# Routing stage of a PEER decoder layer: counts of five heads behind the last query, query 15 in token halves, both look-ups in one run, and the fill of W on ScalarE

## The chip, the cores and the metric

The kernel runs on one core of one Trainium2 chip. A core has a matrix engine (TensorE, here PE, with its weight loads PEld), a vector engine (VectorE, DVE), an activation engine (ScalarE, ACT), a general engine (GpSimd, POOL) and an engine that issues transfers (SyncE, SP). Each works through its own instructions in order and waits on semaphores for the others. The metric is the device time of one execution in microseconds (us), the median of several runs.

## The reference

One decoder layer on 256 tokens of width 2048. Attention (eight differential and eight stick-breaking heads), a product-key expert layer (PEER), and a gated embedding, each with a layer norm behind it. The change lies in the PEER layer, cut to this:

```python
q = (xt @ wq).reshape(t, PEER_HEADS, PEER_QDIM)            # 8 heads, 256 wide
sa = einsum('thc,nc->thn', q[..., :128], sub_keys[0])      # 128 scores for each half
sb = einsum('thc,nc->thn', q[..., 128:], sub_keys[1])
va, ia = top_k(sa, 16)
vb, ib = top_k(sb, 16)
cand = va[..., :, None] + vb[..., None, :]                 # 16 x 16 pairs
cidx = ia[..., :, None] * 128 + ib[..., None, :]
top, sel = top_k(cand, 16)
eidx = take_along_axis(cidx, sel)                          # 16 experts of 16384 per head
gates = softmax(top)
act = gelu(einsum('thed,td->the', u[eidx], x))
out = einsum('the,thed->td', gates * act, v[eidx])
```

## The kernel before, in words

Routing comes first: for each of 16 half-queries `hh` (8 heads, two keys each) `query(hh)` multiplies the 256 tokens with a block of `peer_wq` (16 matmuls of 256 columns, which the profile counts as 32 passes), ACT copies the result to `qT`, and `scores` multiplies it with the keys into `S`. On DVE `best_scores(hh)` finds the 16 best of 128 for two token tiles; with both keys of a head done, `best_pairs` finds the 16 best pairs and turns their places into the two indices of each expert. For that it makes a run of three operations for each key: compare the place with 0 to 15 (`equal`, tile `eqsel`), multiply with the indices found before (`TIh`), add up (`tensor_reduce`), into `iaN` or `ibN`. `head_slots` sends the indices of the first 32 tokens to `eig`.

Then the kernel counts which experts are wanted by which group of 32 tokens. POOL scales the indices (`apart`); PE spreads them (`sets_of`, tile `ps_iS`, the index matmuls); ACT copies them out as `a` and `nb`. DVE turns `a` into one-hot rows `oa` (`hots_out`, one `equal` of 3584 elements), ACT makes 28 rows `sb` of steps with Sign activations (`steps_up`), and `counted` adds their 28 products in `ps_cnt`, for all heads in the same three banks.

What sets the order: most of these instructions are kept in the order in which the program is written. The work behind a query is written as generators that the class `Background` runs at ticks. A tick follows each of the 16 matmuls of a query; `bg.add(work, delay)` makes the work due so many ticks later, and a generator that yields `n` goes on `n` ticks later. `hot_work(h)` is added behind query 2h+2 with a delay of 22+2h: the index matmuls at its start, then Sign rows at a tick each, then the counts, four per tick. After query 15 `bg.flush()` runs what is left. Head 6 is done by hand behind it, and head 7 by `last_hot`, where the compare of `a` and of the last step rows lies on DVE in pieces.

On DVE hots_out(h) stands behind best_scores(2h+3) and ahead of best_pairs(h+1).

Next comes the sorting of experts into blocks. `classes` copies the counts out (`below`), makes flags `f` where an expert is wanted, and combines them by token groups (`wh`, `nn`, `nm`, `I`). `offsets` and `running` add them up on PE (`ps_off`, `ps_run`), `lists` makes the indices `idx` of the experts of a block, and POOL gathers their rows by indirect DMA (`uf`). From there PE transposes each block (`ps_T`, copied by ACT to `uT`) and multiplies it with the tokens, block by block; the gelu goes into `W`, a tile of 42 x 224 elements per partition, which must hold ones before since the gates are multiplied in wherever they come. After that the same is done with the rows of `v`, and the layer ends.

The lines that matter: `query` from L810, `scores` L821, `best_pairs` L845, `hot_tiles` L981, `steps_up` L985, `hot_work` L998, `last_hot` L1018, `classes` L1046, the end of the loop (`bg.flush`) L1464 and the fill of `W` L1491. `W` is filled by one instruction on POOL:

```python
    nc.gpsimd.memset(W, 1.0)
    sorting = classes(flp, cnt, I, some)
    next(sorting)
```

`W` lies where tiles of the routing lay (pools `tk`, `tkl`), so it waits for the last of them, the transfer of head 7's `eg` to `eig`. Pools `lp` (with `I`, `run`, `io`) and `flp` are open beside `hotp` (with `sb`, `apart`), so that their tiles can be filled early. `oa` takes turns in three buffers `gb` that later hold gathered rows.

Of the kernel before, what the change touches and what calls it, by code (L numbers as in the profile page):

```python
# [20 lines left out]
P = 128  # L21
T = 256
# [30 lines left out]
ACT_LAST = 10  # L53
NCB = NKEY + 1
# [242 lines left out]
def build(tc, a, out):  # L297
# [512 lines left out]
    def query(hh):  # L810
        ps = pbank(pq, "ps_q", "q", 3)
        wf = su.load(a["peer_wq"][hh])
        for dt in range(ND):
            keep(nc.tensor.matmul(ps[:, :T], wf[:, dt * P:(dt + 1) * P], XF[:, dt],  # L814
                                  start=dt == 0, stop=dt == ND - 1))
            bg.tick()
        qT = tk.tile([P, T], F32, name="qT", tag="qT", bufs=2)
        keep(nc.scalar.copy(qT, ps[:, :T]))
        bg.add(scores(hh, qT), 2)

    def scores(hh, qT):  # L821
        pk = pbank(pq, "ps_k", "k", 1)
        for t in range(NT):
            keep(nc.tensor.matmul(pk[:, t * NKEY:(t + 1) * NKEY], qT[:, t * P:(t + 1) * P],
                                  keysT[:, hh % 2, :], start=True, stop=True))
        keep(nc.scalar.copy(S[:, hh // 2, :, hh % 2, :],
                            pk[:, :T].rearrange("p (t n) -> p t n", t=NT)))
        yield from ()
# [16 lines left out]
    def best_pairs(h0, n, then=None):  # L845

        q0, nq = NT * h0, NT * n
# [12 lines left out]
        for q in range(q0, q0 + nq):  # L860
            top16(tkl, CV[:, q], CI[:, q], cand[:, q - q0, :])
        ci = CI[:, qs].rearrange("p q k -> p (q k)")
        s4, s2 = (tkl.tile([P, 96], U32, name=nm)[:, :nk] for nm in ("by16", "by4"))
        pF, u1 = (tkl.tile([P, 96], F32, name=nm)[:, :nk] for nm in ("pF", "u1"))
        at = [tkl.tile([P, 96, 2], F16, name=f"at{which}")[:, :nk] for which in range(2)]
        two = [P, nk, 2]
# [10 lines left out]
        keep(nc.vector.scalar_tensor_tensor(
            at[1], pF[:, :, None].to_broadcast(two), -36.0, u1[:, :, None].to_broadcast(two),
            op0=ALU.add, op1=ALU.max))
        for which, dst in ((0, iaN), (1, ibN)):  # L880
            eq = tkl.tile([P, 96, TOPK], F16, name="eqsel", tag="eqsel", bufs=1)[:, :nk]
            equal(eq, io128[:, :TOPK], at[which])
            e4 = eq.rearrange("p (q k) i -> p q k i", k=TOPK)
            keep(nc.vector.tensor_tensor(
                e4, e4, TIh[:, qs, which, None, :].to_broadcast([P, nq, TOPK, TOPK]),
                op=ALU.mult))
            for h in range(n):
                keep(nc.vector.tensor_reduce(
                    dst[:, :, (h0 + h) * TOPK:(h0 + h + 1) * TOPK],
                    eq.rearrange("p (h t k) i -> p h t k i", t=NT, k=TOPK)[:, h],  # L890
                    axis=AX.X, op=ALU.add))
            if then:
                then(which)
        for h in range(h0, h0 + n):
            head_slots(h)
# [100 lines left out]
    hots = {}  # L996

    def hot_work(h, xa, xb):  # L998
# [3 lines left out]
        oa, sb = hot_tiles()  # L1002
        hots[h] = oa[:, :SETS], a2
# [14 lines left out]
    def last_hot(h):  # L1018

        oa, sb = hot_tiles()  # L1020
# [20 lines left out]
        best_pairs(h, 1, then)  # L1041
# [4 lines left out]
    def classes(flp, cnt, I, some):  # L1046

        f = flp.tile([P, 8, P], F16, name="f8")
        keep(nc.vector.memset(f[:, 0], 0.0))
        for ps, g, n in zip(cnt, (0, 3, 6), (3, 3, 1)):  # L1050
            v = ps[:, :n * NCB].rearrange("p (n b) -> p n b", n=n)
            keep(nc.scalar.copy(below[:, g:g + n], v))
            tt(f[:, 1 + g:1 + g + n], v[:, :, 1:], below[:, g:g + n, :P], ALU.is_gt)
        w = f
# [374 lines left out]
    for hh in range(2 * PH):  # L1429
        if hh == HEARLY:  # L1430
# [7 lines left out]
            iaN, ibN = (lsp.tile([P, NT, PH * TOPK], F32, name=nm) for nm in ("iaN", "ibN"))  # L1438
# [3 lines left out]
            lp = pools.open("lp", "right", bufs=1)  # L1442
            flp = pools.open("flp", "right", bufs=1)
# [9 lines left out]
        query(hh)  # L1453
        if hh:
            best_scores(hh - 1)
        if hh and hh % 2 == 0:
# [3 lines left out]
            best_pairs(h, 1)  # L1460
            xs = [apart(h, which, nc.gpsimd) for which in range(2)]
# [29 lines left out]
    nc.gpsimd.memset(W, 1.0)  # L1491
# [5 lines left out]
    for i, (k0, n) in enumerate(spread(K4, KR)):  # L1497
        running(k0, n, "TU"[i], i == 0)
# [814 lines left out]
```

## Time and profile before

| | |
|---|---|
| median of 3 runs | 1500.56 us (1498.18 to 1502.86) |
| the profiled execution | 1506.18 us |
| its span, first to last instruction | 1504.3 us |
| mean granted clock of TensorE | 0.97 |
| PE busy | 1404.7 us (93%) |
| DVE busy | 884.6 us (59%) |
| ACT busy | 656.6 us (44%) |
| POOL busy | 442.7 us (29%) |

Every time below is from one profiled execution, counted from its first instruction. PE is busy nearly all the time, and the two places in the page's row of 40 slices where it is not show where to look: slices 14 and 15, from about 530 to 600 us, with 7 and 4 tenths. The first routing query starts at 416.4 us, the last one's scores end at about 548.7, and the first block of expert rows is gathered at 588.18. In a row of the timeline stand start, duration, engine, line, operation, output and inputs, shapes, the count, and in brackets how long the engine had been idle and what ended that; a row can hold several instructions. In the chain of waits a row is a link: start, duration, what.

### The profile page before, as it was taken

Reading aid. Unit: us, or ns where it says so; the run is one execution under the profiler, and the core shown is the slowest. Engines: PE = TensorE matmul, PEld = TensorE weight load, DVE = VectorE, ACT = ScalarE, POOL = GpSimd, SP = SyncE. Lnnn points to the kernel's source line nnn. Section 1 sums busy time; section 2 is a strip of 40 time slices with the busy share of each in tenths; the row PEclk is TensorE's granted clock in tenths of the full one; section 3 lists DMA queues with packets and bytes.
Section 4 is the critical chain, followed back from the end, with each engine's and each line's share of the span. In section 5 each row is a group of like instructions: output and inputs, shape, how many; then the busy total and the mean of one; then the engine's idle time right before and its main releaser. Section 6 shows DMA issues by size and latency. Waiting matters only on the chain.

```text
span 1504.3 us, 32578 instructions
## 1 busy us (share of the span) xinstructions
PE 1404.7 (93%) x13216; PEld 1109.3 (74%) x13216; DVE 884.6 (59%) x2455; ACT 656.6 (44%) x1447; POOL 442.7 (29%) x413
## 2 busy tenths in 40 slices
PE   9999999999999974998999998999998999995898
PEld 7888888887888863997888887888985444331686
DVE  5456568875558887678856766787532000005767
ACT  5587646875325562543544454444550000003632
POOL 0033213310041114332433443443553444321000
PEclk9999999999999985999999999999999999997899
DMA  8655665548543204878799888999999999999471
GB/s 304 203 167 156 195 212 154 153 149 319 177 162 112 85 1 155 312 286 311 288 376 335 322 305 321 347 368 360 400 396 386 418 417 419 413 382 353 171 264 56
DMA packets 74733, 402.82 MB, mean 268 GB/s; under 512 B 10980, under 2 KB 13060, under 8 KB 36580
## 3 DMA queue, kind: packets, MB, share of 16 engines
q0 software_dynamic: 39280, 272.11, 46.6%
q1 hardware_dynamic: 33568, 125.42, 24.6%
q10 hardware_dynamic: 1728, 3.15, 0.6%
q8 instruction: 105, 1.72, 0.4%
q14 instruction: 52, 0.43, 0.1%
HBM read 404.97 MB, written 4.45 MB: 272 GB/s over the span
## 4 chain that ended last, share of the span: by engine, by line
PE 66%; DMA 11%; issue 10%; DVE 6%; POOL 4%; ACT 1%; POOLq 0%; ACTq 0%; DVEq 0%
PE ps_T L1528 9%; PE ps_qk L336 8%; PE ps_u L1551 7%; PE ps_q L814 7%; PE ps_u L1536 6%; PE ps_qk L338 4%; DMA vf<-v_rows,idx 4%; DMA vg<-v_rows,idx 2%; PE ps_v L355 2%; DMA vx<-v_rows,idx 2%; PE ps_v L357 2%; PE ps_v L356 2%; PE ps_gate L355 2%; PE ps_gate L357 2%; PE ps_gate L356 2%
## 5 line engine op out<-in xcount | busy, mean ns | idle before, releaser
L1530 ACT COPY uT<-ps_T 128x512 f32<-128x512 f32 x404 | 220.9, 615 | 288.5 <-PE ps_T L1528 264.3
L239 DVE TENSOR_TENSOR wl<-wf,wh 128x1024 fp32r<-128x1024 f32 (+1 forms) x167 | 192.9, 1169 | 104.1 <-ACT wh L238 102.6
L1503 POOL DMA_INDIRECT uf<-u_rows,idx x101 | 134.3, 1330 | 281.6 <-PE ps_T L1528 217.4
L1528 PE MATMUL ps_T<-ident,uf 128*128 128x128 f32 x1616 | 211.0, 276 | 0.3 <-issue 0.2
L238 ACT CAST wh<-wf 128x1024 fp32r<-128x1024 f32 (+1 forms) x167 | 155.0, 945 | 115.7 <-PE ps_v L357 34.0
L336 PE MATMUL ps_qk<-X,wh 128*128 128x512 f32 x512 | 185.2, 401 | 0.0
L1528 PEld LDWEIGHTS ps_T<-ident,uf 128*128 128x128 f32 x1616 | 181.5, 146 | 4.1 <-issue 3.3
L338 PE MATMUL ps_qk<-X,wl 128*128 128x256 f32 x512 | 145.7, 285 | 0.0
L1551 PE MATMUL ps_u<-uT,XF 128*32 128x128 f32 x3904 | 134.8, 277 | 9.0 <-issue 7.2
L1536 PE MATMUL ps_u<-XF,uT 128*128 128x128 f32 (+2 forms) x832 | 134.9, 314 | 7.9 <-ACT acts L1600 4.3
L1835 DVE BATCH_NORM_STATS2 st<-ps_v 128x6 f32<-128x512 f32 x8 | 5.6, 700 | 214.0 <-PE ps_v L1871 162.2
L1536 PEld LDWEIGHTS ps_u<-XF,uT 128*128 128x128 f32 x832 | 121.3, 194 | 10.6 <-ACT acts L1600 5.2
L1551 PEld LDWEIGHTS ps_u<-uT,XF 128*32 128x32 f32 x3904 | 105.3, 110 | 29.9 <-issue 21.8
L1788 PE MATMUL ps_v<-vf,W 128*32 128x512 f32 x936 | 107.6, 612 | 16.1 <-DMA vf<-v_rows,idx 16.1
L814 PE MATMUL ps_q<-XF,wf 128*128 128x256 f32 x512 | 121.9, 384 | 0.0
L336 PEld LDWEIGHTS ps_qk<-X,wh 128*128 128x128 f32 x512 | 96.4, 188 | 22.0 <-issue 1.0
L1262 DVE SCALAR_TENSOR_TENSOR junk<-io,ibF,ps_find 128x128 f16<-128x128 f16 x224 | 64.4, 344 | 74.1 <-PE ps_find L1254 61.0
L814 PEld LDWEIGHTS ps_q<-XF,wf 128*128 128x128 f32 x512 | 93.0, 190 | 10.4
L1788 PEld LDWEIGHTS ps_v<-vf,W 128*32 128x32 f32 x936 | 40.2, 111 | 80.8 <-issue 59.8
L1392 DVE SCALAR_TENSOR_TENSOR y<-gb,ew,y 128x2048 f32<-128x2048 f32 x31 | 72.8, 2349 | 45.5 <-DMA gb<-v_rows,eig 45.5
L338 PEld LDWEIGHTS ps_qk<-X,wl 128*128 128x128 f32 x512 | 96.3, 188 | 2.5 <-issue 1.3
L1788 PE MATMUL ps_v<-vx,W 128*32 128x512 f32 x672 | 74.3, 592 | 0.0
(364 smaller groups left out, 2505.0 us busy)
## 6 DMA issues: line engine op xcount, KB each, us to landing
wf<-w_qk SPq DMA_DIRECT2D x64, 512.0 KB
wf<-w_out SPq DMA_DIRECT2D x32, 512.0 KB
wf<-peer_wq SPq DMA_DIRECT2D x16, 1024.0 KB
wf<-ple_gate SPq DMA_DIRECT2D x16, 1024.0 KB
wf<-w_v SPq DMA_DIRECT2D x16, 512.0 KB
wf<-w_sv SPq DMA_DIRECT2D x15, 512.0 KB
iarow<-s_iar SPq DMA_DIRECT2D x14, 512.0 KB
x<-x SPq DMA_DIRECT2D x2, 1024.0 KB
```

What stands on the lines that cost most here:

```text
L238: self.order(nc.scalar.copy(wh, src))
L239: self.order(nc.vector.tensor_tensor(wl, src, wh.bitcast(F32), op=ALU.subtract))
L336: nc.tensor.matmul(ps, wh[:, j * P:(j + 1) * P], xt[:, dt, :], start=dt == 0, stop=False)
L338: nc.tensor.matmul(ps[:, :T], wl[:, j * P:(j + 1) * P], xt[:, dt, :T], start=False, stop=dt == ND - 1)
L814: keep(nc.tensor.matmul(ps[:, :T], wf[:, dt * P:(dt + 1) * P], XF[:, dt], start=dt == 0, stop=dt == ND - 1))
L1392: keep(nc.vector.scalar_tensor_tensor(ys, g, ew[:, j:j + 1], ys, op0=ALU.mult, op1=ALU.add))
L1503: keep(nc.gpsimd.indirect_dma_start(out=dst, out_offset=None, in_=src, in_offset=bass.IndirectOffsetOnAxis(ap=idx[:, col:col + 1], axis=0) ...
L1528: keep(nc.tensor.transpose(ps[:, j * P:(j + 1) * P], rows[i][:, (4 * c + j) * P:(4 * c + j + 1) * P], ident))
L1530: keep(nc.scalar.copy(turned[i][:, c * 512:(c + 1) * 512], ps))
L1536: keep(nc.tensor.matmul(ps[:, :n], uT[:, d * P:(d + 1) * P], groups_of(d, *block.wide), start=d == 0, stop=d == ND - 1))
L1551: keep(nc.tensor.matmul(ps[32 * q:32 * q + 32, w * P:(w + 1) * P], XF[:, d, t0:t0 + 32], uT[:, d * P:(d + 1) * P], start=first and not w, ...
L1788: keep(nc.tensor.matmul(ps[32 * j:32 * j + 32], w, vf[:, j * 512:(j + 1) * 512], start=False, stop=last))
```

## The change

Four edits.

1. The counts of heads 2 to 6 are no longer made by `hot_work` but kept in a list and made in one run of 140 matmuls behind the last scores. For that `sb` has five buffers in place of two, and heads 5 and 6 have an `oa` of their own. Head 6 goes through `hot_work` like the others, and the delays are 20+h in place of 22+2h.
2. Query 15 is made in two halves of 128 tokens, each with its own copy and scores, a tick at every second matmul. hots_out(6) now stands ahead of best_scores(15).
3. In `best_pairs` one run of three operations, twice as wide, finds the indices for both keys, in a common tile `iab`. Head 7 keeps two runs, since its work goes on behind the first.
4. `W` is filled with ones by ACT, in four copies of 2352 elements: two behind the copies of the counts, two behind the first `running`. The flags are made in a function of their own, ahead of the closing of `hotp`; `lp` and `flp` are opened behind it, on the same place, so the small fillings of `I` and `run` on POOL and the load of `io` on SP now stand behind the counts.

The places in the program's order, without times. First PE around query 14, from behind the index matmuls of head 4; `ps_q` are the query, `ps_k` the scores, `ps_cnt` the counts (of head 4, with `oa`), `ps_iS` the index matmuls (with `apart`). Before:

```order
L814 MATMUL ps_q<-XF,wf 128x256 x4
L824 MATMUL ps_k<-keysT,qT 128x128 x2
L814 MATMUL ps_q<-XF,wf 128x256 x16
L824 MATMUL ps_k<-keysT,qT 128x128 x2
L814 MATMUL ps_q<-XF,wf 128x256 x5
L992 LDWEIGHTS oa
L992 MATMUL ps_cnt<-sb,oa 128x129
```

Now:

```order
L818 MATMUL ps_q<-XF,wf 128x256 x10
L829 MATMUL ps_k<-keysT,qT 128x128 x2
L818 MATMUL ps_q<-XF,wf 128x256 x16
L829 MATMUL ps_k<-keysT,qT 128x128 x2
L818 MATMUL ps_q<-XF,wf 128x256 x7
L982 LDWEIGHTS apart
L982 MATMUL ps_iS<-eighth,apart 128x16
```

The counts of head 4 are gone from query 14, and the index matmuls of head 5 stand behind its ninth matmul (two ahead of the scores, seven behind); before they stood behind the sixteenth.

Second, PE at the last query. Before, where the index matmuls of head 5 end and the counts of head 5 begin:

```order
L967 MATMUL ps_iS<-eighth,apart 128x16
L814 MATMUL ps_q<-XF,wf 128x256 x2
L824 MATMUL ps_k<-keysT,qT 128x128 x2
L814 MATMUL ps_q<-XF,wf 128x256 x14
L824 MATMUL ps_k<-keysT,qT 128x128 x2
L992 LDWEIGHTS oa
L992 MATMUL ps_cnt<-sb,oa 128x129
```

Now, from the index matmuls of head 5 to those of head 6:

```order
L982 MATMUL ps_iS<-eighth,apart 128x16
L818 MATMUL ps_q<-XF,wf 128x256 x7
L818 MATMUL ps_q<-XF,wf 128x128 x4
L829 MATMUL ps_k<-keysT,qT 128x128 x2
L818 MATMUL ps_q<-XF,wf 128x128 x16
L829 MATMUL ps_k<-keysT,qT 128x128
L818 MATMUL ps_q<-XF,wf 128x128 x12
L829 MATMUL ps_k<-keysT,qT 128x128
L982 LDWEIGHTS apart
L982 MATMUL ps_iS<-eighth,apart 128x16
```

Query 15 has become 32 narrow matmuls with two scores, and the index matmuls of head 6 follow at once; the 140 counts stand behind these and ahead of the index matmuls of head 7.

Third, ACT behind the last counts (`below` copies them out). Before:

```order
L986 ACTIVATE sb<-ioh,nb 128x129 x10
L1052 COPY below<-ps_cnt 128x387 x2
L1052 COPY below<-ps_cnt 128x129
L1116 CAST run<-ps_run 128x4x128
L1530 COPY uT<-ps_T 128x512 x4
```

Now:

```order
L1004 ACTIVATE sb<-ioh,nb 128x129 x10
L1072 COPY below<-ps_cnt 128x387 x2
L1072 COPY below<-ps_cnt 128x129
L1520 COPY W<-one 128x2352 x2
L1139 CAST run<-ps_run 128x4x128
L1520 COPY W<-one 128x2352 x2
L1562 COPY uT<-ps_T 128x512 x4
```

Two pieces of `W` stand ahead of `run` and two ahead of the first `uT`; on POOL the memset of `W` is gone from between `eig` and the first gather.

The diff, cut to its core:

```diff
+LATER = 2
+OWN_OA = (5, 6)
...
+    def query(hh, step=NT):
         wf = su.load(a["peer_wq"][hh])
-        for dt in range(ND):
-            keep(nc.tensor.matmul(ps[:, :T], wf[:, dt * P:(dt + 1) * P], XF[:, dt],
-                                  start=dt == 0, stop=dt == ND - 1))
-            bg.tick()
...
+        for t0 in range(0, NT, step):
+            c = slice(t0 * P, (t0 + step) * P)
+            ps = pbank(pq, "ps_q", "q", 3)[:, :step * P]
+            for dt in range(ND):
+                keep(nc.tensor.matmul(ps, wf[:, dt * P:(dt + 1) * P], XF[:, dt, c],
+                                      start=dt == 0, stop=dt == ND - 1))
+                if step == NT or dt % 2:
+                    bg.tick()
...
+            bg.add(scores(hh, qT, range(t0, t0 + step)), 2)
...
+        else:
+            equal(eqsel, io128[:, :TOPK], at.rearrange("p w q k two -> p q w k two")
+                  .rearrange("p q w k two -> p (q w) k two"))
+            e4 = eqsel.rearrange("p (qw k) i -> p qw k i", k=TOPK)
             keep(nc.vector.tensor_tensor(
...
+                e4, e4, TIh[:, qs].rearrange("p q w i -> p (q w) i")[:, :, None, :]
+                .to_broadcast([P, 2 * nq, TOPK, TOPK]), op=ALU.mult))
+            keep(nc.vector.tensor_reduce(iab.rearrange("p q w c -> p (q w) c")[:, :, hs], e4,
+                                         axis=AX.X, op=ALU.add))
+        head_slots(h)
...
+    def hot_tiles(h):
+        if h in OWN_OA:
+            oa = hotp.tile([P, SETS, P], F16, name="oa", tag="oa", bufs=len(OWN_OA))
+        else:
+            oa = gin.tile([P, 32, P], F16, name="oa", tag="gb", bufs=NGB)[:, :SETS]
+        return oa, hotp.tile([P, SETS, NCB + 1], F16, name="sb", tag="sb", bufs=PH - LATER - 1)
...
+        if h >= LATER:
+            later.append((h, oa, sb))
+            return
         yield 3
         for s in range(0, SETS, 4):
             counted(h, oa, sb, s, s + 4)
...
-        query(hh)
+        query(hh, NT if hh < 2 * PH - 1 else 1)
...
-            if h < PH - 2:
-                bg.add(hot_work(h, *xs), 22 + 2 * h)
+            best_pairs(h)
+            bg.add(hot_work(h, *(apart(h, which, nc.gpsimd) for which in range(2))), 20 + h)
     bg.flush()
+    hots_out(PH - 2)
     best_scores(2 * PH - 1)
-    last = hot_work(PH - 2, *xs)
-    next(last)
-    hots_out(PH - 2)
-    for _ in last:
-        pass
+    for h, oa, sb in later:
+        counted(h, oa, sb, 0, SETS)
     last_hot(PH - 1)
...
+    flags(f8)
+    pools.close("hotp", "pq")
     pools.close("tk", "tkl")
+    lp = pools.open("lp", "right", bufs=1)
+    flp = pools.open("flp", "right", bufs=1)
...
-    nc.gpsimd.memset(W, 1.0)
-    sorting = classes(flp, cnt, I, some)
+
+    def fill(x0, x1):
+        n = NC * NDT // 4
+        for x in range(x0, x1):
+            keep(nc.scalar.copy(W.rearrange("p c n -> p (c n)")[:, x * n:(x + 1) * n],
+                                one.to_broadcast([P, n])))
+
+    fill(0, 2)
+    sorting = classes(flp, f8, I, some)
     next(sorting)
-    pools.close("hotp", "pq")
...
     for i, (k0, n) in enumerate(spread(K4, KR)):
         running(k0, n, "TU"[i], i == 0)
+    fill(2, 4)
```

More of the change, by code (lines that the diff above doesn't have):

```diff
@@ L843, in best_scores, with best_pairs @@
             top16(tk, TV[:, q, hh % 2, :], TI[:, q, hh % 2, :], S[:, hh // 2, t, hh % 2, :])
-    def best_pairs(h0, n, then=None):
-        q0, nq = NT * h0, NT * n
+    def best_pairs(h, then=None):
+        q0, nq = NT * h, NT
         qs, nk = slice(q0, q0 + nq), nq * TOPK
@@ L861, in best_pairs, with pair @@
             top16(tkl, CV[:, q], CI[:, q], cand[:, q - q0, :])
[L862 to L866, printed above, removed]
+        ci = CI[:, qs]
+        s4, s2 = (tkl.tile([P, nq, TOPK], U32, name=nm) for nm in ("by16", "by4"))
+        pF, u1 = (tkl.tile([P, nq, TOPK], F32, name=nm) for nm in ("pF", "u1"))
+        at = tkl.tile([P, 2 * nk, 2], F16, name="at")
+        at = at.rearrange("p (w q k) two -> p w q k two" if then else
+                          "p (q w k) two -> p w q k two", w=2, k=TOPK)
+        two = [P, nq, TOPK, 2]
+        def pair(x):
+            return x[:, :, :, None].to_broadcast(two)
         keep(nc.gpsimd.tensor_copy(TIh[:, qs], TI[:, qs]))
@@ L874, in best_pairs @@
                                             op0=ALU.mult, op1=ALU.add))
-        keep(nc.vector.scalar_tensor_tensor(pF, at[0][:, :, 0], -4.0, ci,
+        keep(nc.vector.scalar_tensor_tensor(pF, at[:, 0, :, :, 0], -4.0, ci,
                                             op0=ALU.mult, op1=ALU.add))
[L877 to L893, printed above, removed]
@@ L994, in counted @@
                                   stop=h == PH - 1 and (s % 12 == 11 or s == SETS - 1)))
-    hots = {}
+    hots, later = {}, []
     def hot_work(h, xa, xb):
@@ L1001, in hot_work @@
         nb = less(sets_of(xb))
[L1002 to L1003 removed]
+        oa, sb = hot_tiles(h)
+        hots[h] = oa, a2
         yield 1
@@ L1039, in then, with flags @@
                 counted(h, oa, sb, s0, s1)
-        best_pairs(h, 1, then)
+        best_pairs(h, then)
     def tt(out, x, y, op):
         keep(nc.vector.tensor_tensor(out, x, y, op=op))
-    def classes(flp, cnt, I, some):
-        f = flp.tile([P, 8, P], F16, name="f8")
+    def flags(f):
         keep(nc.vector.memset(f[:, 0], 0.0))
@@ L1053, in classes @@
             tt(f[:, 1 + g:1 + g + n], v[:, :, 1:], below[:, g:g + n, :P], ALU.is_gt)
+    def classes(flp, f, I, some):
         w = f
@@ L1437, in build @@
             ibF = lsp.tile([P, T], F32, name="ibF")
-            iaN, ibN = (lsp.tile([P, NT, PH * TOPK], F32, name=nm) for nm in ("iaN", "ibN"))
+            iab = lsp.tile([P, NT, 2, PH * TOPK], F32, name="iab")
+            iaN, ibN = iab[:, :, 0], iab[:, :, 1]
             ian = lsp.tile([P, NT, PH * TOPK], F16, name="ian")
@@ L1441, in build @@
             gate = lsp.tile([P, NT, PH, TOPK], F32, name="gate")
-            lp = pools.open("lp", "right", bufs=1)
-            flp = pools.open("flp", "right", bufs=1)
+            f8 = lsp.tile([P, 8, P], F16, name="f8")
+            one = lsp.tile([P, 1], F32, name="one")
+            nc.gpsimd.memset(one, 1.0)
             hotp = pools.open("hotp", "right", bufs=1)
```

48 lines of the change are left out of this document (26 added, 22 removed).

## The prediction

> **What bounds the kernel now.** The stretch that the change touches lies between the first routing query and the first block of expert rows. I read it in four steps: busy time by stretches, the chain of waits through them, then each engine in order of time. The stretches come first (busy us and count of PE, PEld, DVE, ACT, POOL, then the granted clock, the DMA share and GB/s):
>
> ```profile
> 548.70:567.60 18.90, 6.42 (x66) 5.13 (x63) 17.71 (x69) 11.74 (x42) 5.02 (x6) 0.62 0.02 4
> 567.60:573.00 5.40, 4.59 (x28) 2.92 (x28) 3.57 (x8) 3.76 (x12) 0.58 (x1) 0.50 0.71 255
> 573.00:582.00 9.00, 0.00 (x0) 0.00 (x0) 8.86 (x10) 0.00 (x0) 7.94 (x1) 0.50 0.00 1
> ```
>
> From 548.70 on, DVE is busy 17.71 of 18.90 us and PE a third of it; from 573 to 582 PE and ACT do nothing at all. So behind the queries DVE sets the pace. The chain of waits says when it took over (start, duration, what):
>
> ```profile
> 539.91 2.03 DVE oa L834
> ...
> 575.71 6.13 DVE nn L1069
> ...
> 588.18 6.50 DMA uf<-u_rows,idx
> ```
>
> Ahead of 539.91 the rows of the chain are PE's queries; from there, from the `oa` of hots_out(5), they are DVE's. The first gather of expert rows, at 588.18, ends the stretch. Behind it all gathers and products follow in the same order as before, so what this gather gains, the end should gain.
>
> PE in order of time, where the counts of a head stand among the queries:
>
> ```profile
> 496.22 0.61 PE L824 MATMUL ps_k<-keysT,qT 128*128 128x128 f32 x4
> ...
> 524.01 7.07 PE L814 MATMUL ps_q<-XF,wf 128*128 128x256 f32 x32
> 530.92 0.61 PE L824 MATMUL ps_k<-keysT,qT 128*128 128x128 f32 x4
> ...
> 533.53 0.40 PE L992 MATMUL ps_cnt<-sb,oa 128*128 128x129 f16 x4
> 533.76 0.65 PE L814 MATMUL ps_q<-XF,wf 128*128 128x256 f32 x2
> 534.25 0.40 PE L992 MATMUL ps_cnt<-sb,oa 128*128 128x129 f16 x4
> ...
> 548.66 2.61 PE L992 MATMUL ps_cnt<-sb,oa 128*128 128x129 f16 x28
> ...
> 558.10 3.21 PE L992 MATMUL ps_cnt<-sb,oa 128*128 128x129 f16 x28 [5.91 <-DVE oa L834]
> ```
>
> 32 query matmuls fill 530.92 - 524.01 = 6.91 us, two of them 0.43 us. With four counts between, the pitch is 534.25 - 533.53 = 0.72 us, so four counts cost 0.29 us and a head's 28 cost 2.0 us. Standing in one run they take 2.61 us, or 3.21 us after the clock has fallen.
>
> DVE in order of time, one head:
>
> ```profile
> 539.91 2.03 DVE L834 TENSOR_TENSOR oa<-io,a 128x3584 f16<-128x3584 f16 x1 [2.01 <-ACT a L973]
> ...
> 546.33 0.42 DVE L834 TENSOR_TENSOR eqsel<-io,at 128x512 f16<-128x512 f16 x1
> 546.85 0.43 DVE L884 TENSOR_TENSOR eqsel<-eqsel,TIh 128x512 f16<-128x512 f16 x1
> 547.31 0.69 DVE L888 TENSOR_REDUCE iaN<-eqsel 128x32 f32<-128x512 f16 x1
> ...
> 549.67 0.16 DVE L901 SCALAR_TENSOR_TENSOR eg<-iaN,ibN 32x16 uint32<-32x16 f32 x1
> ...
> 556.03 2.01 DVE L834 TENSOR_TENSOR oa<-io,a 128x3584 f16<-128x3584 f16 x1
> 557.96 0.47 DVE L855 TENSOR_TENSOR cand<-TV 128x96 f32<-128x96 f32 x2
> ...
> 566.52 2.08 DVE L834 TENSOR_TENSOR oa<-io,a 128x1792 f16<-128x1792 f16 x2
> ```
>
> A head costs DVE 1.93 us for hots_out (556.03 to 557.96), 7.83 for best_pairs (541.84 to 549.67) and 6.36 for `eg` and two best_scores (to 556.03): 16.1 us. In front of `oa` it has stood 2.01 us, waiting for `a`. So a head takes 18.1 us, and PE gives that pace: `a` hangs on index matmuls that stand at a fixed place among its queries.
>
> **Part 1, the counts and the new ticks.** Only the counts of heads 2, 3 and 4 stand among queries now; those of 5 and 6 already follow the last one (548.66 and 558.10). So 3 x 2.0 = 6.0 us leave PE's query loop, and its period falls to 16.1 us. The earlier index matmuls (tick 20+h in place of 22+2h, seven ticks of 0.43 us earlier for head 5) take away the wait for `a`: DVE now runs into its own 16 us instead. When does hots_out(5) start? Two things hold it.
>
> ```profile
> 531.57 0.37 ACT L826 COPY S<-ps_k 128x256 f32<-128x256 f32 x1 [0.27 <-PE ps_k L824]
> ```
>
> - Supply: the scores of query 13 (530.92) come 2 x 2.0 us earlier, at 526.9. The copy to S ends 1.0 us behind them (531.94 less 530.92), best_scores(13) takes 6.36 / 2 = 3.2: 531.1.
> - DVE's own work: hots_out(3) can't come before the scores of query 9, whose place no removed count precedes: 496.22 + 1.0 + 3.2 = 500.4. Two heads of 15.55 us (part 2) give 531.5.
>
> The later one decides: 531.5 in place of 539.91. From there to the last best_pairs it is now 557.96 - 539.91 = 18.05 us, and 17.5 with part 2: 549.0 in place of 557.96. **Gain: 9.0 us.** Bounds: with nothing from part 2, 500.4 + 2 x 16.1 + 18.05 gives 550.65, a gain of 7.3; with the most of it (below) supply holds at 531.1 and the gain is 557.96 - 531.1 - 18.05 + 1.6 = 10.4.
>
> The counts themselves now stand in PE's tail: 5 x 28 in one run, 5 x 2.61 = 13.1 us. The last scores, which end where the counts begin now (548.66), end 6.0 us earlier, at 542.6. Then come the index matmuls of head 6, and the counts from 543.3 to 556.4. The index matmul of head 7 queues behind them; `oa` of head 7, which waits for its result, is due on DVE at 549.0 + 8.56 (566.52 less 557.96, the distance from `cand` to `oa` today) = 557.5. So the counts are hidden, with about 0.7 us to spare after the matmul and ACT's copy. The cover is thin: without it every us of counting is a us of time. The halves of query 15 have as many columns in twice as many matmuls: 0 to 6.9 us by the row of 32, the former if columns set the time, as I take it. DVE comes to best_scores(15) only at 531.5 + 1.93 + 7.3 + 3.2 + 1.93 = 545.9, so 3 us of it would be hidden there; the counts have only their 0.7.
>
> The clock in the first fence (0.62 from 548.70, 0.50 from 567.60) shows that PE falls to half speed when it idles. [...]
>
> **Part 2, both look-ups in one run.** Six operations, 546.33 to 549.67 or 3.34 us, become three of twice the width. `oa` gives the rate of such an operation: 3584 elements in 2.03 us against 512 in 0.42, so 0.52 ns per element; 512 more cost 0.27 us for each of the two products. The reduction, at 0.69 us, I give twice as much for its 512 more, 0.53. Its own three starts lie 0.52 and 0.46 apart, and 0.72 is left for it: 0.79 + 0.73 + 1.25 = 2.8 us, a saving of 0.55 per head (bounds 0 to 1.6, half of the six). It counts three times above, where DVE holds the pace; head 7 keeps its two runs.
>
> **Part 3, the fill of W.** Two views side by side, DVE and POOL:
>
> ```profile
> 574.15 1.56 DVE L1044 TENSOR_TENSOR wh<-wh 128x512 f16<-128x512 f16 x4
> 575.62 6.21 DVE L1069 TENSOR_SCALAR nn<-wh 128x128 f16<-128x128 f16 x1
> 581.86 0.22 DVE L1044 TENSOR_TENSOR nn<-nn,wh 128x128 f16<-128x128 f16 x1
> 582.12 0.20 DVE L1069 TENSOR_SCALAR nm<-nn 128x128 f16<-128x128 f16 x1
> ```
>
> ```profile
> 573.85 7.94 POOL L1491 MEMSET W<- 128x9408 f32 x1 [2.86 <-DMA eig<-eg]
> ```
>
> `nn` takes 6.21 us, its twin `nm` 0.20, and `nn` ends at 581.83, 0.04 us behind the memset (573.85 + 7.94 = 581.79). It stands for the memset's length. Without the memset it takes 0.2: **gain 6.0 us**, bounds 0 (if something else holds it) and 6.0.
>
> [...]
>
> What ACT now carries:
>
> ```profile
> L238 ACT CAST wh<-wf 128x1024 fp32r<-128x1024 f32 x127 | 133.0, 1048 | 101.2 <-PE ps_v L357 34.0 <-PE ps_qk L336 29.4 <-DMA wf<-w_out 14.6
> 584.72 0.59 ACT L1116 CAST run<-ps_run 128x512 f16<-128x512 f32 x1 [11.97 <-PE ps_run L1113]
> ```
>
> By the cast's 1.02 ns per element a piece of 2352 costs at most 2.4 us. The first two wait, like the memset, for eig to land (573.85 in today's times) and end by 578.7. `run`, next on ACT, is ready at 584.72 - 6.0 = 578.7: just hidden, at worst some tenths late. The other two follow `run` and end near 584; ACT's next work is `uT`, behind the gather (588.18 + 6.50 - 6.0 = 588.7). They are hidden too, and POOL has nothing in that time but to wait for the lists. That I, run and io now lie where oa and sb lay makes their filling wait for the last counts; the two loads behind SP took at most 5.4 us (the stretch with DMA share 0.71, 0.00 behind it), and `mark` reads io some 7.8 us behind the counts. Hidden.
>
> **Sum.** 9.0 + 6.0 = 15.0 us at the first gather. The profiled execution took 1506.18 us (span 1504.3): 1491.2. The runs' median, 1500.56, is 5.6 us below it, and the gain is a difference, so 1500.56 - 15.0 = **1485.6 us**. Two gathers near 1120 change places; with the spread of the runs (1498.18 to 1502.86) I allow 2 us either way.
>
> **Rivals.**
> - *The counts take the place of the wait.* If PE runs the five heads at half clock, they take 5 x 3.21 = 16.05 us in place of 13.05, end at 559.4, and `oa` of head 7 is 2.3 us late: 1487.9. [...] Against it: PE is busy until 542.6. Chance 0.12.
> - *Only one of the two gains comes.* If `nn` is held by something other than the memset, or the fill on ACT puts the same time in front of `run`, 9.0 us remain: 1491.6. Against it: the two ends 0.04 us apart. Chance 0.09.
> - *The gain is lost later*, in gathers that are bound by the DMA engines and not by when they start. A third of it gone gives 1490.6. Against it: nothing for that stage is fetched before 588.18. Chance 0.08.
> - *Slower: ACT's fill.* ACT works in order, so `uT` stands behind four pieces. They start at 573.85 and would be in time up to (588.7 - 574.4) / 4 = 3.6 us each; from 3.6 + 15.0 / 4 = 7.3 us each the whole gain is gone, and at 9 us the time is about 1507. It needs a copy from one broadcast element to run at 3.1 ns per element, three times the cast's. Chance 0.03.
>
> **How the numbers follow.** The forecast has 0.66, the rivals 0.12, 0.09, 0.08 and 0.03; 0.02 is left for a time within 0.3% (4.5 us, about what a measurement here can tell from no change). Lower end: 15.0 + 0.6 for the clock, 1.4 for part 2 (10.4 in place of 9.0) and 2 for the gathers and the runs: 1481.6, taken to 1481. The upper end takes in the first three rivals: 1492. Faster 0.95, same 0.02, slower 0.03.
>
> **What would show it.** Right: no idle time of DVE in front of `oa`; the last best_pairs about 9 us earlier; the counts of five heads in one run of some 13 us, ended before `oa` of head 7 starts; `nn` at 0.2 us; `run` on ACT without a wait for the fill; the first gather at about 573. Wrong: PE's index matmul of head 7 ending a wait of DVE, pieces of W over 3.6 us, or a last stage that grows by what this one loses.

## The result and the profile after

The changed kernel takes 1484.82 us (median of 6 runs, 1483.16 to 1489.01), the kernel before in the same set 1502.74 (6 runs, 1498.18 to 1505.2). The ratio is 0.9886, with a 95% interval of 0.9866 to 0.9907: 14 to 20 us less. The profiled execution took 1483.16 us with a span of 1481.4. One of the later traces, that of `after_pool_fill`, was taken at a clock of 0.835; from it only rows of DVE and POOL are read.

To compare traces I use one **distance**: from the first matmul of the first query to the first gather of rows of u. It contains all that the change touches. Up to `nn` it comes again to 0.03 us: `nn` starts 159.27 us behind the first query in all four traces that have the routing of the kernel before untouched, and 150.56 to 150.59 us behind it in four of the changed kernel and its variants. What follows `nn` varied by 1.4 us in the kernel before, for a reason shown below, and by 0.03 in the changed one. The distance was 588.18 - 416.35 = 171.83 us and is 571.75 - 414.62 = 157.13: **14.70 us less**. The first query itself starts 1.73 us earlier, ahead of everything that was edited; where a time of the changed kernel is set against one of before, I add these 1.73.

The stretches of the changed kernel, in the columns of the prediction's first fence:

```profile
542.00:551.00 9.00, 8.62 (x140) 8.04 (x137) 8.49 (x39) 8.49 (x29) 0.36 (x1) 1.00 0.01 3
551.00:554.00 3.00, 0.00 (x0) 0.00 (x0) 2.72 (x11) 0.00 (x0) 0.00 (x0) 1.00 0.00 0
554.00:557.00 3.00, 0.45 (x4) 0.27 (x4) 2.84 (x5) 0.70 (x4) 1.17 (x2) 0.57 0.09 19
...
562.00:572.00 10.00, 3.48 (x31) 2.54 (x30) 7.56 (x32) 7.94 (x7) 0.25 (x1) 0.50 0.03 14
```

The stretch from 573 to 582 us in which PE and ACT did nothing while DVE stood is gone: between the last head's counts and the gather PE, DVE and ACT all have work. The counts of five heads fill 542 to 551 at a granted clock of 1.00. Behind them PE idles for nearly four us, which is spare. Now the chain of waits of the changed kernel (start, duration, what):

```profile
530.17 1.92 DVE oa L839
...
542.73 1.93 DVE oa L839
...
559.82 1.80 PE ps_cnt L1010 x15
561.64 0.49 ACT below L1072
...
565.29 0.12 DVE nn L1092
...
571.75 6.47 DMA uf<-u_rows,idx
```

`nn` was a link of 6.13 us and is one of 0.12. DVE is still what sets the end, up to the last head's counts. PE in order of time:

```profile
541.79 8.99 PE L1010 MATMUL ps_cnt<-sb,oa 128*128 128x129 f16 x140
554.72 0.22 PE L982 MATMUL ps_iS<-eighth,apart 128*128 128x16 f16 x2 [3.93 <-POOL apart L972]
556.24 0.22 PE L982 MATMUL ps_iS<-eighth,apart 128*128 128x16 f16 x2 [1.30 <-DVE apart L972]
557.24 4.79 PE L1010 MATMUL ps_cnt<-sb,oa 128*128 128x129 f16 x28 [0.78 <-DVE oa L839]
```

140 counts take 8.99 us, 0.064 each on the average (0.059 from one to the next, but 0.24 to 0.29 for the last three, each 0.05 us behind the end of a row of ACT's `sb`), and PE then idles for 3.93 us until the last head's indices come. DVE in order of time: two `oa` of the loop, between them the wide look-ups, at the end `nn` and `nm`:

```profile
498.69 2.01 DVE L839 TENSOR_TENSOR oa<-io,a 128x3584 f16<-128x3584 f16 x1
...
505.25 0.69 DVE L839 TENSOR_TENSOR eqsel<-io,at 128x1024 f16<-128x1024 f16 x1
506.04 0.69 DVE L905 TENSOR_TENSOR eqsel<-eqsel,TIh 128x1024 f16<-128x1024 f16 x1
506.77 1.22 DVE L908 TENSOR_REDUCE iab<-eqsel 128x64 f32<-128x1024 f16 x1
508.02 0.16 DVE L916 SCALAR_TENSOR_TENSOR eg<-iab 32x16 uint32<-32x16 f32 x1
...
514.39 2.00 DVE L839 TENSOR_TENSOR oa<-io,a 128x3584 f16<-128x3584 f16 x1
...
565.21 0.19 DVE L1092 TENSOR_SCALAR nn<-wh 128x128 f16<-128x128 f16 x1
...
565.69 0.20 DVE L1092 TENSOR_SCALAR nm<-nn 128x128 f16<-128x128 f16 x1
```

No `oa` waits for `a` any more, and a head takes 514.39 - 498.69 = 15.70 us in place of 18.2. `nn` takes 0.19. ACT, which now fills `W`:

```profile
564.40 4.20 ACT L1520 COPY W<-one 128x2352 f32<-128x2352 f32 x2 [2.06 <-DMA eig<-eg]
568.51 0.58 ACT L1139 CAST run<-ps_run 128x512 f16<-128x512 f32 x1
568.99 4.20 ACT L1520 COPY W<-one 128x2352 f32<-128x2352 f32 x2
579.41 0.59 ACT L1562 COPY uT<-ps_T 128x512 f32<-128x512 f32 x1 [6.23 <-PE ps_off L1120]
```

A piece takes 2.10 us. `run` follows two of them without a gap, and the other two are over 6.23 us before the first `uT`.

The spans differ by 22.9 us and the distances by 14.7. Of the rest, 1.7 us lie ahead of the first query, and 10.1 between the first gather and the first product with rows of v (558.86 us before, 548.72 after); behind that the changed kernel takes 3.6 us more. Whether these belong to the change was asked below.

### The profile page after: what moved, and what is told of

It reads as the page before. It is cut to its first block, busy times and chain, and to the rows that moved or that the text cites. A ratio compares the mean times of both kernels' runs of the same rounds, so it can differ in the third digit from the quotient of the medians.

```text
span 1481.4 us, 32627 instructions
## 1 busy us (share of the span) xinstructions
PE 1398.7 (94%) x13248; PEld 1136.8 (77%) x13248; DVE 875.3 (59%) x2434; ACT 665.8 (45%) x1453; POOL 443.2 (30%) x413
## 4 chain that ended last, share of the span: by engine, by line
PE 66%; DMA 16%; DVE 8%; issue 6%; POOL 2%; ACT 1%; POOLq 0%; ACTq 0%; DVEq 0%
PE ps_T L1560 11%; PE ps_qk L338 8%; PE ps_u L1583 8%; DMA vf<-v_rows,idx 7%; PE ps_u L1568 7%; PE ps_q L818 5%; PE ps_qk L340 4%; DMA vx<-v_rows,idx 3%; DMA vg<-v_rows,idx 3%; DMA gb<-v_rows,eig 2%; PE ps_v L357 2%; PE ps_v L358 2%; PE ps_v L359 2%; PE ps_gate L357 2%; PE ps_gate L358 2%
## 5 line engine op out<-in xcount | busy, mean ns | idle before, releaser
L1568 PE MATMUL ps_u<-XF,uT 128*128 128x128 f32 (+2 forms) x832 | 131.3, 309 | 5.4 <-ACT W L1648 2.7
L1820 PE MATMUL ps_v<-vf,W 128*32 128x512 f32 x936 | 109.5, 616 | 18.2 <-DMA vf<-v_rows,idx 18.2
L818 PE MATMUL ps_q<-XF,wf 128*128 128x256 f32 (+1 forms) x544 | 117.7, 369 | 0.0
L1820 PEld LDWEIGHTS ps_v<-vf,W 128*32 128x32 f32 x936 | 53.0, 112 | 71.4 <-DMA vf<-v_rows,idx 25.2
L818 PEld LDWEIGHTS ps_q<-XF,wf 128*128 128x128 f32 x544 | 96.1, 190 | 10.7
```

What stands on the lines that cost most here:

```text
L818: keep(nc.tensor.matmul(ps, wf[:, dt * P:(dt + 1) * P], XF[:, dt, c], start=dt == 0, stop=dt == ND - 1))
L1568: keep(nc.tensor.matmul(ps[:, :n], uT[:, d * P:(d + 1) * P], groups_of(d, *block.wide), start=d == 0, stop=d == ND - 1))
L1820: keep(nc.tensor.matmul(ps[32 * j:32 * j + 32], w, vf[:, j * 512:(j + 1) * 512], start=False, stop=last))
```

## The experiments

Every kernel ran beside the kernel before on the same chip, in three sets on three chips; the third set's chip is some 25 us faster for both, so times are compared within a set. The table gives each distance, its change against 171.83, and the ratio of times to the kernel before, with what it is in us (one less the ratio, times the median of the kernel before in that set: 1506.04, 1502.96 or 1476.25 us).

| kernel | distance, us | change | ratio (95%) | us less in time |
|---|---|---|---|---|
| before_act_fill | 165.82 | -6.0 | 0.9954 (0.9936 to 0.9971) | 6.9 |
| before_pool_pieces | 166.57 | -5.3 | 0.9973 (0.9955 to 0.9991) | 4.1 |
| before_ticks_only | 169.31 | -2.5 | 0.9970 (0.9956 to 0.9984) | 4.5 |
| before_again | 173.24 | +1.4 | 1.0001 (0.9988 to 1.0013) | -0.1 |
| after_counts_in_loop | 162.14 | -9.7 | 0.9929 (0.9902 to 0.9956) | 10.7 |
| after_pool_fill | not read | | 0.9944 (0.9924 to 0.9963) | 8.4 |
| after_old_ticks | 159.11 | -12.7 | 0.9922 (0.9898 to 0.9945) | 11.7 |
| after_two_lookups | 158.06 | -13.8 | 0.9921 (0.9898 to 0.9943) | 11.9 |
| after_whole_query15 | 157.47 | -14.4 | 0.9902 (0.9877 to 0.9928) | 14.7 |
| after_fill_at_once | 161.50 | -10.3 | 0.9918 (0.9897 to 0.9939) | 12.1 |
| after_again | 157.10 | -14.7 | 0.9902 (0.9883 to 0.9920) | 14.5 |
| after_later_one | 155.47 | -16.4 | 0.9899 (0.9879 to 0.9920) | 14.9 |

The time agrees with the distance within 2 us in every row; in the first comparison, of the result, it was 17.1 against 14.7. The intervals are 2 to 4 us to either side, so what one small edit is worth is read from the distance alone.

### The fill of W alone, and put back

The kernel before with the fill on ACT, by the change's own `fill` (and a tile `one` for it):

```diff
-    nc.gpsimd.memset(W, 1.0)
...
     sorting = classes(flp, cnt, I, some)
     next(sorting)
+    fill(0, 2)
...
     for i, (k0, n) in enumerate(spread(K4, KR)):
         running(k0, n, "TU"[i], i == 0)
+    fill(2, 4)
```

> The kernel before, with the fill of W alone moved to ACT (two copies of 2352 elements behind the copies of the counts, two behind the first running). Measure: time from the first query matmul to the first gather of expert rows, 171.83 us before and 157.13 after. If POOL's memset holds nn: nn takes 0.2 us, the measure falls by 6.0 to 165.8, and the time by about 6 (0.4%). Rival, nn is held by something else, or the fill on ACT costs what it saves: the measure stays within 1 us of 171.8.

The distance is 165.82 us, 6.0 less, and DVE shows in place of the 6.21 us:

```profile
572.39 0.19 DVE L1069 TENSOR_SCALAR nn<-wh 128x128 f16<-128x128 f16 x1
```

So this part is worth 6.0 us by itself. The other way round, the changed kernel with a memset on POOL in place of the four copies:

```diff
-    fill(0, 2)
+    nc.gpsimd.memset(W, 1.0)
...
-    fill(2, 4)
```

> The changed kernel with W filled by one memset on POOL again, in front of the three short memsets. If the memset holds nn: nn takes about 6 us and the measure rises by 6.0 to 163.1; the short memsets of I and run now stand behind it and could add to it only if PE or ACT need them, 0 to 0.5 us. Rival: with DVE earlier the memset no longer meets nn, or something else held it: 157 to 158.

The time falls by 8.4 us only, where the changed kernel's falls by 14.5 to 17.1 (ratios 0.9902 and 0.9886). First POOL's row of the fill, then DVE's rows of `nn` and what follows:

```profile
612.58 7.93 POOL L1523 MEMSET W<- 128x9408 f32 x1 [4.39 <-DMA eig<-eg]
```

```profile
612.83 7.73 DVE L1092 TENSOR_SCALAR nn<-wh 128x128 f16<-128x128 f16 x1
620.60 0.23 DVE L1065 TENSOR_TENSOR nn<-nn,wh 128x128 f16<-128x128 f16 x1
```

`nn` starts 0.25 us behind the memset and stands for the rest of it, here 7.73 us and not the 6 that I expected. The distance of 163.1 can't be read from this trace; by the ratios the memset costs the changed kernel 6.1 to 8.7 us.

### What nn stands for: the memset cut in pieces

In the kernel before, POOL fills W in 14 instructions of 672 elements, and nothing else is altered:

```diff
-    nc.gpsimd.memset(W, 1.0)
+    for x in range(14):
+        keep(nc.gpsimd.memset(W[:, 3 * x:3 * x + 3], 1.0))
```

> The kernel before, with the fill of the weights' tile still on GpSimd but in 14 pieces of 3 columns of 112... each a fourteenth of the tile, instead of one instruction; the whole computation is done. Same distance (171.83 us in the kernel before, 165.82 with the fill on ACT). [...]

POOL, then DVE:

```profile
571.81 8.78 POOL L1492 MEMSET W<- 128x672 f32 x14 [2.48 <-ACT below L1052]
```

```profile
573.97 0.35 DVE L1069 TENSOR_SCALAR nn<-wh 128x128 f16<-128x128 f16 x1
...
578.47 1.52 DVE L1124 TENSOR_SCALAR mark<-io,off 128x128 f16<-128x128 f16 x6
```

The fill takes 8.78 us in place of 7.94, and `nn` still starts inside it, but takes 0.35 us. It ends at 574.31, 0.05 us behind the end of one piece (574.27), as in the kernel before it ended 0.04 behind the end of the memset. So it stands for one instruction of POOL (0.63 us from one to the next), not for the fill, which goes on to 580.59; what holds it that long is not shown. What is left of the cost shows at `nm`, 0.35 us in place of 0.20, and at `mark`, 1.52 in place of 1.06. The distance is 166.57 us, 0.75 more than with the fill on ACT.

### The counts back in the loop

The changed kernel, with the counts of heads 2 to 4 among the queries again:

```diff
-        if h >= LATER:
+        if h >= 5:
             later.append((h, oa, sb))
             return
```

> The changed kernel with the counts of heads 2, 3 and 4 among the queries again (those of 5 and 6 stay behind the last one). If the counts on PE hold DVE: PE's period per head is 17.8 us and not 15.75, DVE waits in front of oa for a, hots_out(5) starts 5.0 us later against the first query and the measure is 162.1. Rival, the earlier ticks of the index matmuls alone made the gain and the counts are beside the path: 157 to 158.

The distance is 162.14 us, 5.0 more than in the changed kernel. The waits in front of `oa` are back on DVE:

```profile
517.84 2.02 DVE L839 TENSOR_TENSOR oa<-io,a 128x3584 f16<-128x3584 f16 x1 [0.66 <-ACT a L988]
...
535.62 2.03 DVE L839 TENSOR_TENSOR oa<-io,a 128x3584 f16<-128x3584 f16 x1 [1.39 <-ACT a L988]
```

535.62 - 517.84 = 17.78 us a head: PE gives the pace. The counts in the loop are what made DVE wait.

### The ticks alone, and put back

The kernel before with delays of 20+h in place of 22+2h:

> The kernel before with the delays 20+h in place of 22+2h and nothing else. The index matmuls of head 5 come 7 ticks (3.0 us) earlier on PE, the counts still stand in the loop: DVE's wait for a shrinks from 2.0 us, hots_out(5) starts 3.0 us earlier, measure 168.8. Rival, the ticks carry the whole gain of the query stage: 9 to 10 us earlier, 162. Other rival, PE's period alone decides and the ticks do nothing: 171.8.

The distance is 169.31 us, half a us more than expected. The `oa` of head 5 and the last `cand` come 3.04 us earlier, as expected; what is missing went into `nn`, which stood 6.72 us here and not 6.21. POOL, then DVE:

```profile
570.62 7.94 POOL L1491 MEMSET W<- 128x9408 f32 x1 [3.38 <-DMA eig<-eg]
```

```profile
571.88 6.72 DVE L1069 TENSOR_SCALAR nn<-wh 128x128 f16<-128x128 f16 x1
```

The changed kernel with the old delays:

```diff
-bg.add(hot_work(h, ...), 20 + h)
+bg.add(hot_work(h, ...), 22 + 2 * h)
```

> The changed kernel with the old due times of the background work (22 + 2h in place of 20 + h); the whole computation is done. Measured is the distance from the first matmul of the first query to the first gather of the rows of u: 171.83 us in the kernel before, 157.13 in the changed one. My theory: the sixth hot_work block (oa of head 5) starts at 117.5 instead of 115.5 us behind the first query, since the first two blocks' starts are set by the due times and the rest is DVE's cycle of 15.7 us; everything behind it moves by the same 2.0 us: 159.1. Rival: PE's tail with the counts of five heads, and not DVE's chain, is what the gather waits for; then nothing moves before DVE's delay has used up PE's spare: 157.1. A second rival: the due times decide in each cycle, as PE's ticks come later; then up to 7 us: 164.

159.11 us, as forecast, with the waits of DVE short but in every cycle:

```profile
500.37 2.02 DVE L839 TENSOR_TENSOR oa<-io,a 128x3584 f16<-128x3584 f16 x1 [0.43 <-ACT a L988]
...
516.56 2.02 DVE L839 TENSOR_TENSOR oa<-io,a 128x3584 f16<-128x3584 f16 x1 [0.43 <-ACT a L988]
```

With 22+2h the index matmuls come 34 ticks apart, and PE does that in 16.19 us, half a us more than DVE needs.

### The look-ups in two runs

The changed kernel with the look-ups of both keys apart for all heads, on the same common tile:

```diff
-        at = at.rearrange("p (w q k) two -> p w q k two" if then else
+        at = at.rearrange("p (w q k) two -> p w q k two" if True else
...
-        if then:
+        if True:
             for which in range(2):
...
-                then(which)
+                if then:
+                    then(which)
```

> The changed kernel with the look-ups of both keys in two runs for all heads, as before the change; the whole computation is done. Same distance (157.13 us in the changed kernel). My theory: DVE's cycle becomes 16.1 us instead of 15.7, and each of the cycles that stand between the first block and the last head's pairs adds its part: 5 or 6 times 0.43 us less what the first cycles wait for anyway, so +1.3 to +2.6: 158.4 to 159.7. Rival: the look-ups of the early heads run beside waits of DVE, and only the last one or two count: +0.4 to +0.9, 157.5 to 158.0. Should the place of the counts alone have made the whole gain: 157.1.

158.06 us, 0.93 more. My theory asked for 1.3 to 2.6 and falls; it is its rival, just above its upper edge of 158.0, and with three heads at 0.31 us each in place of one or two at 0.43. The start of the first three cycles is the same to 0.01 us as in the changed kernel, since DVE waits for scores there; only the last two cycles (16.01 us in place of 15.70 each) and the way to the last `cand` (0.31) count. DVE's rows of one head:

```profile
504.45 0.23 DVE L887 SCALAR_TENSOR_TENSOR at<-pF,u 128x64 f16<-128x64 f32 x1
504.59 0.42 DVE L839 TENSOR_TENSOR eqsel<-io,at 128x512 f16<-128x512 f16 x1
...
507.08 0.69 DVE L899 TENSOR_REDUCE iab<-eqsel 128x32 f32<-128x512 f16 x1
507.80 0.16 DVE L917 SCALAR_TENSOR_TENSOR eg<-iab 32x16 uint32<-32x16 f32 x1
```

From `eqsel` to `eg` it is 3.21 us, and 2.77 with the wide ones. But the first narrow compare starts 0.14 us behind its `at`, the wide one 0.26 behind: it needs both keys' places. That leaves 0.31 a head.

### Query 15 whole

```diff
-        query(hh, NT if hh < 2 * PH - 1 else 1)
+        query(hh)
```

> The changed kernel with the last query made whole (512 tokens in one accumulation), not by token halves of 128; the whole computation is done. Same distance (157.13 us in the changed kernel). My theory: DVE is the engine that is late from the second block on, and its last top-16 blocks find their scores waiting, so that the time from which the first tile's scores are there does not decide: 157.1, within 0.4. Rival: the split lets DVE begin on the first tile of the last key while PE still makes the rest; then the last best_pairs start later by the part of the query that DVE must wait for, up to 3 matmul groups, 2 to 3 us: 159 to 160.

157.47 us, 0.34 more, within what my theory allowed. All of DVE's rows up to `nn` are where they were (`nn` at 150.56 us from the first query, 150.59 in the changed kernel). The 0.34 us come from ACT:

```profile
564.81 4.20 ACT L1520 COPY W<-one 128x2352 f32<-128x2352 f32 x2 [3.05 <-DVE nn L1092]
568.92 0.58 ACT L1139 CAST run<-ps_run 128x512 f16<-128x512 f32 x1
```

Counted from the first query (414.07 in this trace) `run` starts at 154.85 us, 0.96 later than in the changed kernel (568.51 - 414.62 = 153.89), because the fill in front of it started later by as much. So `run` has some 0.6 us of spare. That the halves of query 15 gain nothing is shown; what starts the fill is not the row named there, since DVE's `nn` was no later, but as in the changed kernel, most likely, the landing of `eig`.

### The fill in one stretch

The changed kernel with all four pieces ahead of `run`:

```diff
-    fill(0, 2)
+    fill(0, 4)
...
-    fill(2, 4)
```

> The changed kernel with all four pieces of the fill of the weights' tile at the first place on ACT, ahead of the class sums' run, and none behind it; the whole computation is done. Same distance (157.13 us). My theory: ACT takes the pieces in its order, 2.1 us each; its copy of ps_run into run then starts at 572.8 instead of 568.5 by the clock of the changed kernel's trace, and the marks' matmuls wait for it: +4.0, 161.1. Rival: ACT's copy of run has spare, or the tile's wait for the DMA of eig sets it: 157 to 158.

161.50 us, 4.4 more:

```profile
566.41 8.31 ACT L1520 COPY W<-one 128x2352 f32<-128x2352 f32 x4 [2.96 <-DVE wh L1065]
574.62 0.57 ACT L1139 CAST run<-ps_run 128x512 f16<-128x512 f32 x1
```

From the first query (415.74) `run` is at 158.88, 4.99 us later than in the changed kernel; the gather loses 4.37 of them. The difference, 0.62, is the spare of `run` again. So it is part of the gain that no more than two pieces stand ahead of `run`.

### Both kernels again

> The changed kernel again, nothing altered. Two numbers: the distance from the first query to the first gather, 157.13 us in the first trace, and the distance from there to the first product with v, 548.72 us. My theory: the first comes again within 0.4, and the second, which was 558.86 us in the kernel before and 553.4 to 558.3 us in other kernels that leave that stretch alone, comes out nearer to 554, since its difference between the two first traces is from run to run. Rival: the changed kernel is really faster by some 5 to 10 us behind the first gather; then 549 again.

> The kernel before again, nothing altered. The distance from the first query to the first gather comes again at 171.8 us within 0.4; the distance from there to the first product with v, 558.86 us in the first trace, comes out at 554 to 557 if its difference to the changed kernel is from run to run, and at 559 again if it belongs to the kernel.

The changed kernel again: 157.10 us. From there to the first product with v it is 525.48 us, and in the kernel before again 526.26: 0.8 us apart, where the first two traces had 10.1 (548.72 and 558.86). Two other kernels of this set have 528.72 and 538.49, and on the chips of the two sets before seven lie between 550.84 and 558.29, in no order that follows their edits. So nothing in the runs gives the 10 us of the first two traces to the change; what makes that stretch longer or shorter stays open. My figure of 554 missed both, as this chip is faster in that stretch. Behind it, up to the end, the eight traces of the changed kernel and its variants (without that of `after_pool_fill`) have 357.1 to 361.4 us and the five of the kernel before and its variants 357.3 to 359.9, so the 3.6 us are not shown to be the change's either. The ratio, 0.9902, is 11.8 to 17.3 us of this set's 1476.25.

The distance of the kernel before did not come again within 0.4: it was 173.24 us. POOL, then DVE:

```profile
573.09 7.98 POOL L1491 MEMSET W<- 128x9408 f32 x1 [4.73 <-DMA eig<-eg]
```

```profile
573.00 0.19 DVE L1069 TENSOR_SCALAR nn<-wh 128x128 f16<-128x128 f16 x1
573.23 0.22 DVE L1044 TENSOR_TENSOR nn<-nn,wh 128x128 f16<-128x128 f16 x1
573.49 7.63 DVE L1069 TENSOR_SCALAR nm<-nn 128x128 f16<-128x128 f16 x1
```

The transfer of `eig` landed later, so the memset began 0.09 us behind `nn`. `nn` got through, and so did the `tensor_tensor` behind it, inside the memset. The next `tensor_scalar`, `nm`, was caught and stood 7.63 us. Against this trace of the kernel before the changed one gains 16.1 us, and not 14.7: what the memset cost depends on the execution.

### A version that goes on

One head more behind the queries; head 4 gets an own `oa`, and `below` takes a tile of the ring of `sb`:

```diff
-LATER = 2
-OWN_OA = (5, 6)
+LATER = 1
+OWN_OA = (4, 5, 6)
...
+        below = hotp.tile([P, NG, NCB], F32, name="below", tag="sb", bufs=PH - LATER - 1)
```

> The changed kernel with the counts of one head more (six, heads 1 to 6) behind the last query; head 4 gets an own oa tile, and the tile below is taken from the ring of sb to make room. The whole computation is done. Distance from the first query to the first gather: 157.13 us in the changed kernel. My theory: the counts of head 1 stand in PE's way between 475.4 and 480.4 and make DVE wait 1.24 us for scores in the cycle of head 1 and about 0.4 us in the next; both go, and the oa of head 5 starts at about 113.9 instead of 115.47. PE's tail becomes 168 counts of 0.064 us, 10.8 us, which still ends before the last head's apart comes (3.9 us of spare in the changed kernel, 0.5 here): 155.5. Rival: PE's tail becomes the bound, since the spare is smaller than the profile shows; then 157 to 159. Second rival: with PE at work nearly until the last head's counts, their 28 matmuls run at the full clock and not at 0.50: then up to 1 us less, 154.5.

155.47 us, as forecast. PE's tail, and two `oa` on DVE:

```profile
538.59 9.98 PE L1010 MATMUL ps_cnt<-sb,oa 128*128 128x129 f16 x168
551.51 0.21 PE L982 MATMUL ps_iS<-eighth,apart 128*128 128x16 f16 x2 [2.93 <-POOL apart L972]
```

```profile
463.86 2.02 DVE L839 TENSOR_TENSOR oa<-io,a 128x3584 f16<-128x3584 f16 x1
...
479.76 2.01 DVE L839 TENSOR_TENSOR oa<-io,a 128x3584 f16<-128x3584 f16 x1
```

This cycle takes 15.90 us; in the changed kernel it took 17.06. 168 counts take 9.98 us and still leave 2.93 of spare, more than the 0.5 that I had reckoned. The second rival falls: the last head's counts, from 554.03 on, had a granted clock of 0.50. By the distance this version beats both kernels, by 1.63 us against the changed one. By the time it can't be told from it: 1462.57 us against 1462.25 in the same set, and a gain of 1.6 us lies within the intervals. Its one trace has the longest way from the first gather to the first product with v of the set, 538.49 us.

## Why the prediction was right

1485.6 us was forecast and 1484.82 measured, and at the first gather 15.0 us were forecast and 14.70 found. The mechanism of both gains held; that the two times lie within 0.8 us is luck, as the last point says. By its steps:

- **hots_out(5).** Forecast 531.5 us; it is 530.09 + 1.73 = 531.8. Of the two things that could hold it, DVE's own work did. The fixed point of that sum, hots_out(3) at 500.4 behind the scores of query 9, is 498.69 + 1.73 = 500.42. From there to 530.09 DVE has no wait. PE's own period, from one pair of index matmuls to the next, is now 15.76 us (512.85 to 528.61), and `a` is ready at 529.05, 1.04 us ahead of its `oa`: PE is by now as slow as DVE, and a saving on DVE alone that is larger than this would bring the waits back.
- **The last best_pairs.** Forecast 549.0, a gain of 9.0; the gain is 8.5 (133.10 us from the first query in place of 141.61), and 0.2 more on the way to `nn`. What was mis-sized is part 2's saving: a head takes 15.70 us, not 15.55. Without a wait it was 16.1 before, so 0.4 were saved a head and not 0.55; the look-ups by themselves bring 0.31, and where the other 0.1 comes from is not shown.
- **The counts in PE's tail.** Mis-sized, on the safe side: 8.99 us and not 13.1, with 3.93 us of idle PE behind them and not 0.7. I took 0.093 us a count from the row of 28 at 548.66 us; the run of 140 shows 0.064. In the trace before, ACT was still making the last six of that head's `sb` beside it:

```profile
549.13 1.87 ACT L986 ACTIVATE sb<-ioh,nb 128x129 f16<-128x129 f16 x6
```

  The counts of that row start 0.059 us apart up to the 24th; the last three start 0.29 apart, each 0.05 to 0.06 us behind the end of one of ACT's rows of `sb`, of which six take 1.87 us, 0.31 each. So the end of the row that I priced with was paced by ACT, not by PE. In `after_later_one`, where ACT ends its `sb` at 547.31, 1.26 us ahead of the counts' end, 168 counts take 9.98 us, 0.059 each.
- **Clock.** No run shows the 0.6 us that the lower end of the range takes for the clock: the 28 counts of the last head ran at 0.50, here and in `after_later_one`. Nor did the rival of half clock for the five heads come: their stretch has 1.00. The clock did fall while PE idled, but not as soon as it idled: behind the 140 counts that took 3.66 us, to 554.45.
- **nn.** Forecast 0.2 us and 6.0 of gain; both found, and isolated by `before_act_fill`. The size holds for this trace of the kernel before: in `before_again` the memset cost 7.4.
- **ACT.** At most 2.4 us a piece forecast, 2.10 found; `run` was forecast "just hidden, at worst some tenths late", and so it is: it starts 1.27 us behind the first of its matmuls, and 1.06 before, so the fill held it for 0.2 us. It has 0.6 us of spare, by two runs. The slower rival is far off: it needed 7.3 us a piece.
- **POOL's short memsets** of `I` and `run`, which now stand behind the counts, took 0.2 us each at 560.6 us, ahead of `nn` (565.21).
- **From the sum to the time.** 15.0 was taken from the shown median, 1500.56 us. Of six runs it is 1502.74, and from there the sum would have given 1487.7. The time fell by 17.1 to 17.9 us (by the ratio, by the medians), 2 to 3 more than the sum. The two differences cancel, so the nearness of 1485.6 to 1484.82 is luck; the sum is borne out by the 14.70 us at the gather. The profiled span fell by 22.9 us, 8.2 more than the distance; in the repeats it fell by 12.4, 3.7 less than the distance, so the excess varies by more than its size.

Put back one by one, the counts cost 5.0 us, the ticks 2.0, the look-ups 0.9 and the halves of query 15 at most 0.3; the fill, taken alone, is worth 6.0. That is 13.9 to 14.3 of the 14.7.

## What to carry to other kernels

When one engine's instruction is many times longer than its twin and ends with another engine's, cut the other instruction in pieces or move it: 14 pieces gave back 5.3 of the 6.0 us without a change of engine. Work of the pace-giving engine that only the end needs belongs behind the pace-giving stretch, up to the spare there; take the duration of such a run from a row that waits for nothing, or it comes out half as long again (0.093 us a count in place of 0.064). And compare two traces over the stretch that the edit touches: here the whole spans differed by 8 us more than that stretch did, and the repeats did not show these 8 us again.

## What the runs showed of the hardware

- What POOL's memset of `W` cost DVE went by when it started, and here a DMA decided that: in every trace with the one memset the landing of `eig` ended POOL's idle time in front of it. Started 1.77 us ahead of the `tensor_scalar` it cost 6.21 us of standing, 1.26 ahead 6.72 (`before_ticks_only`), 0.25 ahead 7.73, and 0.40 ahead of `nm` 7.63: each pair adds up to 8.0, and the memset took 7.93 to 7.98. So an edit that brings DVE's chain forward and leaves the fill behind it can lose part of its gain, as `before_ticks_only` did: 0.5 of 3.04 us.
- A `tensor_tensor` of 0.22 us ran inside the memset of `before_again`, and the same one took 0.22 us in the kernel before, behind its memset. The four `tensor_tensor` that make `wh` took 1.56 us inside the memset of the kernel before and 1.56 ahead of it in `before_again`.
- The granted clock did not fall a fixed time behind the last long run of matmuls. In the changed kernel that run ended at 550.78, and the stretch from 551 to 554 us, with PE idle, still has 1.00; the clock fell at 554.45, 3.66 us behind the run. In the kernel before it ended at 551.27, and 553 to 554 us has 0.67 already, though two pairs of index matmuls of 0.21 us lie in between (551.42 and 551.98). In `after_later_one` it ended at 548.57, with two such pairs behind it (551.51 and 553.02), and 552 to 553 us still has 1.00, 553 to 554 us 0.90. What decides when it falls was not tried.
